# V turned on VectorE in a hybrid attention block on one core of a Trainium2

## The chip, the cores and the metric

The kernel runs on one core of one Trainium2 chip. The time is device microseconds of one execution, the median of several runs. A profile is one further execution, recorded by the hardware profiler. In its rows PE is TensorE, DVE VectorE, ACT ScalarE, POOL GpSimd and SP SyncE; L460 is line 460 of the kernel. All arithmetic is float32 or, for matrix operands, fp32r. Each product is made of three matmuls from a high and a low part of each operand (high × high, high × low, low × high).

## The reference, cut to what matters

One decoder layer with sequence 1024 and width 2048. A combined projection gives q, k, v and a gate for 8 stick-breaking heads (head dim 128) and 8 differential heads (two 64-wide q/k pairs, 128-wide v, rotary on a quarter of q and k). Each group's output is gated with SiLU, both are concatenated and projected, and a gated embedding and a final norm follow.

```python
hn = rmsnorm(h, norm_mix_g[i])
proj = hn @ w_in[i]                       # 1024x2048 @ 2048x8192
sb_q, sb_k, sb_v, sb_g, df_q, df_k, df_v, df_g = jnp.split(proj, split_at, axis=-1)
# stick-breaking: w = exp(log_sigmoid(z) + later), strictly causal; out = w @ v
# differential:   a = softmax1 - lam * softmax2, causal;             out = a @ v
df_out = rmsnorm(df_out, subln_g[i], 1e-5) * (1.0 - lambda_init)
mixed = jnp.concatenate([sb_out * silu(sb_g), df_out * silu(df_g)], axis=-1)
h = h + mixed @ w_out[i]
gate = sigmoid(rmsnorm(h, norm_ple_g[i]) @ w_ple_gate[i])
h = h + gate * (p[i] @ w_ple_proj[i])
return rmsnorm(h, norm_final_g)
```

The row norm is a factor per token, so v and the gate are projected from x times the gain alone and multiplied by the token's factor later.

## The kernel before

Activations lie feature by token: a tile holds 128 features in its partitions and 512 tokens (half a sequence, "half 1" and "half 0") along its free dimension. The kernel has four stages.

**Projection of v and gate (0 to about 650 us).** Class `Seven` computes it with seven instead of eight block products (a Strassen-like scheme). A unit u is one 128-column block, for v and gate and both halves. There are two phases over the inner dimension; phase 0 stores results into `vg_d` in DRAM and phase 1 adds to them there. In `prod` one product is 12 matmuls; `step` then makes a coming product's weight (`whigh` forms a difference on VectorE, L764, and casts it on ScalarE, L799; `wlow` makes the low part on VectorE, L811/L813) and runs what is due (`soon`, `xq`). Results leave PSUM in `evict` (L1017), in the loop over pairs (L1205 to L1217), in `second_result` (L1237), in `rest_of` (L1175) and after S3 (L1257); `vput` (L935) stores them through GpSimd's queue. Block 0 of `vg_d` is v, block 1 the gate; the half comes first. Tiles named `hc` share a ring of four buffers, "f".

**Heads (650 to about 1690 us).** For half 1 and then half 0, sixteen heads each: first the differential heads 8 to 15, then the stick-breaking heads 0 to 7. `unit` computes q and k of one head in four pieces with 96 matmuls and 32 ticks. `Side` holds the previous head's attention as functions with a due tick; `side.tick` runs them between matmuls. The tables at the top (`SC`, `TT`, `SVG`, `VGD`, `SBT`, `NORM_LAT` and others) are these due ticks, in steps of three matmuls. The orders of TensorE, VectorE and ScalarE follow the program text ("manual schedule"); those of GpSimd and of the DMA queues come from the scheduler. `load_vg` (L1505) fetches v and gate of a head; `normed` multiplies them by the tokens' factors `rstd`; `values` (L455) transposes v on TensorE in four 128x128 blocks into PSUM and splits it into high and low parts, token by feature. `turn` and `mix` transpose the attention weights and multiply them with v. For a differential head `norm` (L565) follows, with `roots` on ScalarE and `step` on VectorE. In half 0 the keys and values of half 1 come back as `k2` and `v2` (L1651 to L1664). `wprep` (L170) brings the weights: most heads' high and low parts lie ready in DRAM; those of the last two pieces of head 15 and of heads 0 to 7 in half 1 are made from a raw load (`high`, `low`, L188 to L195).

**Output projection (about 1690 to 2000 us).** `Seven` again, in two phases; in phase 1 the results are stored, summed (`sums`, L1782) and squared (`row_squares`, L1390, whose additions run on GpSimd, L1404).

**Gate, embedding and final norm (to the end).**

Of the kernel before, what the change touches and what calls it, by code (L numbers as in the profile page):

```python
# [20 lines left out]
P = 128  # L21
# [4 lines left out]
H = 8  # L26
# [8 lines left out]
SC = ((6.5, 7, 9.0, 11.5, 15.5, 17.5, 20.0, 21.5), (10.5, 10.5, 15.5, 22.5))  # L35
TT = ((19, 31, 17.5), (20.5, 36.5, 18))
# [3 lines left out]
LV = ((2.5, 2.5), (1, 2))  # L40
LT = ((1, 1), (1, 2.0))
LM = ((0.5, 2.0, 3, 5), (1.5, 2.5, 4.5, 6.5))
LN = ((1, 3.0), (1, 4.5))
PRIO = 300
NORM_LAT = ((11.0, 7.0), (13, 11))
XLAT = 5
SBB = ((20, 20, 15, 15.5, 16, 16.5, 16.5, 16.0), (20, 9, 5.5, 4, 4.5, 6.0, 5.5, 3.5))
SBS = ((-1, 3.5, 15.5, 23.5), (-2.5, 3, 7.0, 11.5))
# [5 lines left out]
ROPE = ((-1.4, 1.5, 3.0, 3.5, 2.7, 4.5, 6.0, 7.0), (-1.9, -1, 0, 1, 0.20000000000000018, 2, 3, 4))  # L54
ROPE_ = ((3.5, 4.0, 6.0, 10.0, 11.6, 12.5, 15.0), (6.5, 7, 9.5, 12.5, 12.6, 13.5, 14))
VGD = ((31, 37, 37.0, 39.0, 41.0), (22.5, 32.5, 35.5, 37.0, 45.0))
# [4 lines left out]
LAST = ((1.5, 4), (2, 4.0))  # L61
# [9 lines left out]
def _body(ctx, nc, tc, ap):  # L71
# [24 lines left out]
    lam = const.tile([P, 1], F32, name="lam", tag="lam")  # L96
    qzs = {}
# [72 lines left out]
    def wprep(wsrc, pc, half, hd):  # L170
# [22 lines left out]
        def low():  # L193
            V.tensor_tensor(lo, raw, hi.bitcast(F32), op=ALU.subtract)
            nc.sync.dma_start(wlo_d[hd, pc].bitcast(F32), lo.bitcast(F32))  # L195
# [111 lines left out]


    def attention(at, pz, half, hd, q, qz, K, KL, VV, sg, vg, state):
# [145 lines left out]
        def values():  # L455

            assert "v" in state
            vps = pp.tile([P, 4, P], F32, name="vps", tag="t")
            for j in range(4):
                T.transpose(vps[:, j, :], vg[0][:, j * P:(j + 1) * P], ident)  # L460
            v = at.tile([P, 2, 4, P], F32R, name="v", tag="v")
            side.later(1 if sb else LV[half][0], lambda: A.copy(v[:, 0], vps))

            def low():
                V.tensor_tensor(v[:, 1], vps, v[:, 0].bitcast(F32), op=ALU.subtract)
                VV.insert(0, v)
                if half == 1:
                    G.dma_start(v_d[hd], v.rearrange("p a b c -> p (a b c)"))

            side.later(2 if sb else LV[half][1], low)  # L470

# [93 lines left out]
        def norm(pr):  # L565
# [12 lines left out]
            def roots():  # L578
# [3 lines left out]
                A.activation(r, r, AF.Exp, scale=-0.5)  # L582

            def step():
                V.scalar_tensor_tensor(sg, sg, -0.5, r, op0=ALU.mult, op1=ALU.mult)
                A.activation(r, r, AF.Square)
# [36 lines left out]
    with tc.tile_pool(name="at", bufs=2) as at, ExitStack() as banks:  # L623
# [32 lines left out]
        class Seven:  # L656

            def __init__(self, w, n, flow):
# [7 lines left out]
                self.extra, self.ticks = (), False  # L666
# [166 lines left out]
            def step(self, taken=None):  # L833

                self.slot += 1
                self.whigh()
                if taken and not self.ticks:
                    taken()
# [95 lines left out]

        def vput(o, ph, hf, blk, u):  # L935
# [81 lines left out]
        def evict(n, u):  # L1017
            pool, tag, m = spots[u] if n == 3 else (ev, "f", 4)
            o = pool.tile([P, HALF], F32, name="s1", tag=tag, bufs=m)
            if u in (3, 5) and n == 3:  # L1020
# [154 lines left out]
        def rest_of(st_, first):  # L1175
# [6 lines left out]
            vput(o, ph, hf, blk, u)  # L1182
# [22 lines left out]
        for u in range(H, 2 * H, 2):  # L1205
            pair = []
            for nm in ("A11", "A12"):
                for j in range(2):
# [4 lines left out]
                    A.copy(o, pair[j])  # L1213
                    if nm == "A11":
                        G.dma_start(vgpart_d[u + j], o)
                    else:
                        vput(o, 0, 1, 0, u + j)  # L1217
        prev = None
        for ph in range(2):
            for u in range(2 * H):  # L1220
# [16 lines left out]
                def second_result():  # L1237
                    prod(u, ph, "A12", a, False)
                    o = ftile()
                    A.copy(o, a)  # L1240
# [56 lines left out]
        side.add([(4, norms)])  # L1297
        X0 = {}
# [79 lines left out]
        def gate_loads(nm, i0, n=4, eng=nc.sync):  # L1378
            e = [(op.slot + (3 if nm in ("A11", "A12") else 2), gate_operand(nm, i0 + j, eng)) for j in range(n)]
# [108 lines left out]
        for half in (1, 0):  # L1488
# [5 lines left out]
            for hd in (ORDER0, ORDER1)[half]:  # L1494
# [10 lines left out]
                def load_vg(vg=vg, hd=hd, half=half):  # L1505
                    for i in range(2):
                        vg.append(f32t(("vf", "gf")[i]) if hd < H else ev.tile([P, HALF], F32, name=("vf", "gf")[i], tag="xt", bufs=4))
                        with tc.issue_after(lastw[0].ins):
                            nc.sync.dma_start(vg[i], vg_d[half, i, hd])
# [47 lines left out]

                acc = two_accs()
                if sb:
# [18 lines left out]
                    def normed(i, vg=vg, rstd=rstd, state=state):  # L1578
                        V.tensor_tensor(vg[i], vg[i], rstd, op=ALU.mult)
# [8 lines left out]
                else:  # L1588
# [50 lines left out]
                    def normed(i, vg=vg, rstd=rstd, state=state):  # L1639
                        V.tensor_tensor(vg[i], vg[i], rstd, op=ALU.mult)  # L1640
# [781 lines left out]
```

## Time and profile before

| | us |
|---|---|
| median of 3 runs (lowest to highest) | 2362.04 (2360.44 to 2363.05) |
| profiled execution, its own time | 2361.19 |
| its span, first to last instruction | 2359.4 |
| TensorE busy | 2317.2 (98%) |
| VectorE busy | 1789.8 (76%) |
| ScalarE busy | 1189.0 (50%) |
| GpSimd busy | 327.3 (14%) |

The mean granted clock of TensorE was 0.997. In a group's row stand the line, engine, operation, the tile written and the tiles read, the shapes and the count; behind the first bar the busy time and the mean length of one in ns; behind the second how long the engine stood idle before such instructions, and what ended the idle time. A row of waits reads "who, on what: total us, times, longest us". Matmuls overlap one another, so a busy time is the union of their lengths.

### The profile page before, as it was taken

How to read it: one execution, taken by the hardware profiler on the slowest of the kernel's cores; microseconds unless marked ns; L12 is line 12 of the kernel's file. 1: busy time of each engine (PE TensorE's matmuls, PEld its weight loads, DVE VectorE, ACT ScalarE, POOL GpSimd, SP SyncE). 2: the span in 40 equal slices, each digit the busy share in tenths (PEclk: the TensorE clock that was granted, in tenths of full speed). 3: DMA queues.
4: the chain of work that ended last, by engine and by line, in shares of the span. 5: the costliest groups of instructions: out<-in, count | busy, mean ns of one | idle time of the engine just before them, and what ended most of it. 6: DMA issues, size and time to landing. Idle time of an engine off the chain costs nothing.

```text
span 2359.4 us, 32445 instructions
## 1 busy us (share of the span) xinstructions
PE 2317.2 (98%) x11096; PEld 1928.3 (82%) x11096; DVE 1789.8 (76%) x3123; ACT 1189.0 (50%) x2214; POOL 327.3 (14%) x480
## 2 busy tenths in 40 slices
PE   9999999999999999999999999999999999999997
PEld 7888888888888878887888888888878878788886
DVE  7489676666677787777888876767887877788778
ACT  6334243333367775445676764445633435533544
POOL 2211112332200000000001011011121232000000
PEclk9999999999999999999999999999999999999998
DMA  7699589999977788787656566677888778898666
GB/s 260 225 313 344 170 255 281 293 278 271 303 246 252 246 266 299 256 263 245 204 182 199 165 190 215 203 214 238 213 211 215 242 229 269 291 326 292 243 227 217
DMA packets 252725, 581.02 MB, mean 246 GB/s; under 512 B 28496, under 2 KB 41040, under 8 KB 252560
## 3 DMA queue, kind: packets, MB, share of 16 engines
q1 hardware_dynamic: 177952, 394.34, 49.7%
q0 software_dynamic: 55312, 149.71, 24.2%
q10 hardware_dynamic: 19296, 34.90, 4.3%
q8 instruction: 87, 1.43, 0.3%
q14 instruction: 78, 0.64, 0.1%
HBM read 373.32 MB, written 213.91 MB: 249 GB/s over the span
## 4 chain that ended last, share of the span: by engine, by line
PE 71%; DVE 12%; ACT 7%; DMA 6%; issue 3%; SPq 0%; ACTq 0%; DVEq 0%
PE acc L263 7%; PE acc L261 7%; PE acc L262 7%; PE pbc L708 6%; PE pbc L710 6%; PE pbc L709 6%; PE pa L708 2%; PE pa L710 2%; PE pa L709 2%; PE tp L480 2%; DMA wraw<-w_out 2%; PE pb L708 1%; PE pb L710 1%; PE pb L709 1%; PE pb L1941 1%
## 5 line engine op out<-in xcount | busy, mean ns | idle before, releaser
L799 ACT CAST wpr<-T 128x512 fp32r<-128x512 f32 x208 | 125.3, 621 | 440.3 <-DVE T L764 360.4
L261 PE MATMUL acc<-xh,whi 128*128 128x512 f32 x768 | 315.0, 410 | 0.0
L263 PE MATMUL acc<-xh,wlo 128*128 128x512 f32 x768 | 302.5, 394 | 1.5 <-DMA wlo<-wlo_d 1.4
L262 PE MATMUL acc<-xl,whi 128*128 128x512 f32 x768 | 301.0, 392 | 0.0
L263 PEld LDWEIGHTS acc<-xh,wlo 128*128 128x128 f32 x768 | 144.5, 188 | 36.2 <-DMA wlo<-wlo_d 3.6
L262 PEld LDWEIGHTS acc<-xl,whi 128*128 128x128 f32 x768 | 145.4, 189 | 24.0
L261 PEld LDWEIGHTS acc<-xh,whi 128*128 128x128 f32 x768 | 145.0, 189 | 23.4 <-DVE qk L1567 0.2
L799 ACT CAST wpr<-wraw 128x512 fp32r<-128x512 f32 x144 | 88.6, 618 | 146.9 <-DMA wraw<-w_vg 40.2
L813 DVE TENSOR_TENSOR wpr<-T,wpr 128x512 fp32r<-128x512 f32 x208 | 145.8, 701 | 9.2 <-ACT wpr L799 6.8
L936 POOL DMA_DIRECT2D vg_d<-hc x120 | 86.8, 724 | 328.4 <-DVE hc L1181 187.9
L503 DVE TENSOR_TENSOR awl<-tp,awh 128x256 fp32r<-128x256 f32 (+1 forms) x160 | 92.5, 578 | 42.8 <-ACT awh L498 42.2
L498 ACT CAST awh<-tp 128x256 fp32r<-128x256 f32 (+1 forms) x160 | 80.6, 504 | 82.6 <-PE tp L480 76.3
L813 DVE TENSOR_TENSOR wpr<-wraw,wpr 128x512 fp32r<-128x512 f32 x144 | 97.7, 686 | 23.5 <-ACT wpr L799 23.5
L321 DVE CUSTOM_DVE_ANT_0 z<-z,masks 128x512 f32<-128x512 f32 (+7 forms) x128 | 97.1, 769 | 23.0 <-PE z L341 14.0
L708 PE MATMUL pbc<-cS,wpr 128*128 128x512 f32 x288 | 112.0, 389 | 0.0
L709 PE MATMUL pbc<-cS,wpr 128*128 128x512 f32 x288 | 112.0, 389 | 0.0
L710 PE MATMUL pbc<-cS,wpr 128*128 128x512 f32 x288 | 112.0, 389 | 0.0
L373 DVE TENSOR_TENSOR_SCAN st<-pt 128x511 f32<-128x511 f32 (+3 forms) x64 | 86.7, 1354 | 27.2 <-ACT pt L366 26.8
L366 ACT ACTIVATE pt<-z 128x512 f32<-128x512 f32 (+3 forms) x64 | 41.8, 653 | 76.6 <-DVE z L349 74.6
L528 PE MATMUL av<-awl,v 128*128 128x256 f32 x256 | 73.4, 287 | 1.7 <-DVE awl L503 1.7
L526 PE MATMUL av<-awh,v 128*128 128x256 f32 x256 | 72.0, 281 | 0.7 <-ACT awh L498 0.7
L527 PE MATMUL av<-awh,v 128*128 128x256 f32 x256 | 72.2, 282 | 0.0
(589 smaller groups left out, 6816.5 us busy)
## 6 DMA issues: line engine op xcount, KB each, us to landing
wlo<-wlo_d SPq DMA_DIRECT2D x94, 512.0 KB, 5.2
whi<-whi_d SPq DMA_DIRECT2D x74, 512.0 KB, 4.1
wraw<-w_vg SPq DMA_DIRECT2D x129, 256.0 KB, 4.8
vg_d<-hc POOLq DMA_DIRECT2D x120, 256.0 KB, 5.7
wraw<-w_in SPq DMA_DIRECT2D x54, 512.0 KB, 5.3
wraw<-w_gate SPq DMA_DIRECT2D x92, 256.0 KB, 4.9
wraw<-w_out SPq DMA_DIRECT2D x72, 256.0 KB, 4.6
wlo_d<-wlo SPq DMA_DIRECT2D x34, 512.0 KB, 3.4
```

What stands on the lines that cost most here:

```text
L261: T.matmul(acc[c], hi[:, k2, kh, c, :], xh, start=first, stop=False)
L262: T.matmul(acc[c], hi[:, k2, kh, c, :], xl, start=False, stop=False)
L263: T.matmul(acc[c], lo[:, k2, kh, c, :], xh, start=False, stop=last)
L321: V.tensor_tensor_reduce(z, z, mwide[:, 0:n], -DF_SCALE, 3.0e38, ALU.add, ALU.min, mx)
L373: V.tensor_tensor_scan(st[:, off + 1:nkey], pt[:, off:nkey - 1], pt[:, off:nkey - 1], initial=1.0, op0=ALU.mult, op1=ALU.bypass)
L503: V.tensor_tensor(wl[:, o, :], tp[:, o, :], wh[:, o, :].bitcast(F32), op=ALU.subtract)
L708: T.matmul(o, wh[:, w], xh, start=start and k == 0, stop=False, skip_group_check=True)
L709: T.matmul(o, wh[:, w], xl, start=False, stop=False, skip_group_check=True)
L710: T.matmul(o, wl[:, w], xh, start=False, stop=k == 3, skip_group_check=True)
L799: A.copy(t[:, 0], src)
L813: V.tensor_tensor(t[:, 1], src, t[:, 0].bitcast(F32), op=ALU.subtract)
L936: G.dma_start(vg_d[hf, blk, u], o, **(dict(accum_op=ALU.add) if ph else {}))
```

## The change

**V is turned on VectorE.** Before it is stored, each tile of v (128 features by 512 tokens) goes through `vturn`: VectorE turns each 32x32 block and puts block (b, k) at place (k, b). Where ScalarE copied a result out of PSUM (`evict` for n > 3, the A12 results of the pairs, `second_result`), VectorE now turns it out of PSUM. In `rest_of` for the first result, the sum is written as before and turned into a second "f" tile two slots later, which is then stored. `load_vg` fetches v in four DMAs of 32 partitions each, in runs of 128 floats, so that it arrives token by feature. `values` no longer uses TensorE or PSUM; it casts and subtracts from the loaded tile. Since tokens are now in the partitions, v is multiplied by a column of factors, `rcol`, made once for each half by four transposes (`columns`, in the first unit). The gate is handled as before.

**Roots.** In `norm`, exponential and square both run in `roots` on ScalarE, into a separate tile; `step` on VectorE uses them.

**Six low parts.** `low` in `wprep` runs on GpSimd for heads 15 and 0 of half 1.

**Order.** Many due steps in the tables are moved. For the differential heads of half 0 from the third on, `k2` and `v2` are requested at steps 13 and 22 of their own unit instead of at its end. In phase 1 of the output projection the function handed to `prod` runs ahead of `whigh`, the last S1's sum is handed over that way, and the second half of `sums` comes one slot later. The first S2 loads of the gate stage are split one slot later.

```diff
-SC = ((6.5, 7, 9.0, 11.5, 15.5, 17.5, 20.0, 21.5), (10.5, 10.5, 15.5, 22.5))
-TT = ((19, 31, 17.5), (20.5, 36.5, 18))
+SC = ((6.5, 7, 9.0, 11.5, 15.5, 17.5, 20.0, 21.5), (10.5, 10.5, 15.5, 23.0))
+TT = ((19, 31, 16.0), (21.5, 36.5, 20))
...
-LN = ((1, 3.0), (1, 4.5))
+LN = ((1, 6.0), (1, 4.5))
...
-NORM_LAT = ((11.0, 7.0), (13, 11))
+NORM_LAT = ((8.0, 8.5), (13, 11))
...
-SBT = ((15, 31, 13), (16.0, 30.0, 11.5))
+SBT = ((15, 31, 13), (16.0, 30.0, 14.5))
...
-SVG = ((18, 37.5, 40, 40, 46), (34.5, 38.5, 41.0, 42.0, 49.5))
-CST = (19.5, 20)
+SVG = ((18, 37.5, 40, 40, 46), (30.5, 37.5, 41.0, 43.5, 49.5))
+CST = (16.5, 19.5)
...
-VGD = ((31, 37, 37.0, 39.0, 41.0), (22.5, 32.5, 35.5, 37.0, 45.0))
+VGD = ((19.5, 37, 37.0, 39.5, 44.0), (22.5, 32.5, 35.5, 37.0, 45.0))
...
+LOWG = ORDER1[H - 1:H + 1]
...
         def low():
-            V.tensor_tensor(lo, raw, hi.bitcast(F32), op=ALU.subtract)
+            (G if half and hd in LOWG else V).tensor_tensor(lo, raw, hi.bitcast(F32), op=ALU.subtract)
...
+    def blocks(t):
+        return t.rearrange("p (b k j) -> p b k j", b=4, k=4)
...
         def values():
-            vps = pp.tile([P, 4, P], F32, name="vps", tag="t")
-            for j in range(4):
-                T.transpose(vps[:, j, :], vg[0][:, j * P:(j + 1) * P], ident)
             v = at.tile([P, 2, 4, P], F32R, name="v", tag="v")
-            side.later(1 if sb else LV[half][0], lambda: A.copy(v[:, 0], vps))
+            hi, lo = [v[:, i].rearrange("p k (b j) -> p b k j", b=4) for i in range(2)]
+            raw = blocks(vg[0])
+            A.copy(hi, raw)
...
-                A.activation(r, r, AF.Exp, scale=-0.5)
+                sqs["root"] = ev.tile([P, HALF], F32, name="root", tag="ssq", bufs=1)
+                A.activation(sqs["root"], r, AF.Exp, scale=-0.5)
+                A.activation(r, sqs["root"], AF.Square)
...
-                A.activation(r, r, AF.Square)
...
+        def vturn(o, src):
+            V.transpose(blocks(o).rearrange("p b k j -> p k b j"), blocks(src))
...
+            if n > 3:
+                vturn(o, aa[u])
...
             V.tensor_tensor(o, o_, t, op=ALU.add)
-            vput(o, ph, hf, blk, u)
+            if not first:
+                return vput(o, ph, hf, blk, u)
+            def turned():
+                v = ftile()
+                vturn(v, o)
+                vput(v, ph, hf, blk, u)
+            if ph == 1 and u == 2 * H - 1:
+                turned()
+            else:
+                gv.soon.append((gv.slot + 2, turned))
...
+        def columns(hf):
+            ps = pp.tile([P, 4, P], F32, name="rps", tag="t")
+            for j in range(4):
+                T.transpose(ps[:, j, :], rstds[hf][:, j * P:(j + 1) * P], ident)
+            side.later(1, lambda: A.copy(rcol[:, hf, :], ps[:, :, 0]))
+        side.add([(20, partial(columns, 1)), (24, partial(columns, 0))])
...
-                            nc.sync.dma_start(vg[i], vg_d[half, i, hd])
+                            if i:
+                                nc.sync.dma_start(vg[i], vg_d[half, i, hd])
+                            for a in range(0 if i else 4):
+                                rows = slice(32 * a, 32 * a + 32)
+                                nc.sync.dma_start(vg[i][rows].rearrange("p (b e) -> p b e", b=4), vg_d[half, i, hd].rearrange("(b p) (a e) -> a p b e", b=4, a=4)[a])
...
+                            r = rcol[:, half, :].rearrange("p (b k j) -> p b k j", b=1, j=1)
+                            V.tensor_tensor(blocks(vg[i]), blocks(vg[i]), r.broadcast_to([P, 4, 4, 32]), op=ALU.mult)
...
-                    op.soon.extend((op.slot + lag + i, fn) for i, fn in enumerate(sums(...)))
+                    op.soon.extend((op.slot + lag + (1 + (lag == 1)) * i, fn) for i, fn in enumerate(sums(...)))
```

More of the change, by code (lines that the diff above doesn't have):

```diff
@@ L468, in low @@
                     G.dma_start(v_d[hd], v.rearrange("p a b c -> p (a b c)"))
-            side.later(2 if sb else LV[half][1], low)
+            side.later(1, low)
         def turn(pr, g):
@@ L1556, in gated, with load_second @@
                     V.tensor_tensor(sg, sg, vg[1], op=ALU.mult)
+                second = {}
+                if half == 0 and not sb and hd not in ORDER0[:2]:
+                    def load_second(nm, d, second=second, hd=hd):
+                        t = at.tile([P, 8 * P], F32R, name=nm, tag=nm)
+                        G.dma_start(t, d[hd])
+                        second[nm] = t
+                    side.add([(13, partial(load_second, "k2", k_d)), (22, partial(load_second, "v2", v_d))])
                 acc = two_accs()
```

75 lines of the change are left out of this document (46 added, 29 removed).

## The prediction

> **What bounds the kernel now.** I read the page's busy line and its chain of waits first.
>
> ```profile
> PE 2317.2 (98%) x11096; PEld 1928.3 (82%) x11096; DVE 1789.8 (76%) x3123; ACT 1189.0 (50%) x2214; POOL 327.3 (14%) x480
> ...
> PE 71%; DVE 12%; ACT 7%; DMA 6%; issue 3%; SPq 0%; ACTq 0%; DVEq 0%
> ```
>
> TensorE works through 98% of the span and carries most of the chain; its idle time is 2359.4 − 2317.2 = 42.2 us. A microsecond of matrix work removed is therefore worth nearly a microsecond, as long as no other engine falls behind. Busy time by stretches shows who could:
>
> ```profile
> 0.00:600.00 600.00, 595.69 (x2614) 491.10 (x2615) 426.90 (x646) 242.97 (x403) 137.52 (x223) 1.00 0.87 269
> ...
> 120.00:160.00 40.00, 40.00 (x178) 33.14 (x177) 34.04 (x56) 15.70 (x28) 6.51 (x12) 1.00 0.92 304
> 160.00:200.00 40.00, 40.00 (x178) 33.10 (x177) 36.80 (x59) 16.51 (x29) 9.23 (x17) 1.00 1.00 355
> 200.00:240.00 40.00, 40.00 (x178) 33.14 (x177) 35.33 (x58) 16.77 (x29) 4.88 (x9) 1.00 0.88 310
> ...
> 2330.00:2359.00 29.00, 14.35 (x100) 12.77 (x98) 20.95 (x46) 9.08 (x16) 0.00 (x0) 0.79 0.48 160
> ```
>
> The columns are TensorE, weight load, VectorE, ScalarE and GpSimd, then clock and DMA. VectorE (fourth number) is the next in line: 71% in the first 600 us, but 92% from 160 to 200. Of the 42.2 us, 14.7 lie in the last 29 us, which the change does not touch. TensorE's own waits, longest first:
>
> ```profile
> PE pbc L708 <- DVE u L1912: 3.5, 4, 1.5
> PE z L427 <- ACT et L439: 3.3, 4, 1.7
> PE acc L261 <- DVE qk L1567: 2.8, 1, 2.8
> ...
> PE acc L263 <- DVE wlo L194: 1.5, 1, 1.5
> ```
>
> The columns are the sum, how often and the longest. With 600 − 595.7 = 4.3 us in the first stretch, 42.2 − 14.7 − 4.3 = 23.2 us of waiting lie between 600 and 2330.
>
> **Step 1, transposes leave TensorE.** The change removes the four transposes of each of 32 calls of values(). Matmuls overlap, so I price a call by the starts around it, not by the length of one (columns: start, length, engine, line):
>
> ```profile
> 657.10 0.39 PE L263 MATMUL acc<-xh,wlo 128*128 128x512 f32 x1
> 657.33 0.60 PE L460 MATMUL vps<-ident,vf 128*128 128x128 f32 x4
> 657.69 0.48 PE L261 MATMUL acc<-xh,whi 128*128 128x512 f32 x1
> 658.00 0.40 PE L262 MATMUL acc<-xl,whi 128*128 128x512 f32 x1
> ```
>
> A 128x512 matmul starts 0.23 us after the last one. The L262 at 658.00 would put its predecessor's undisturbed start at 657.77, and the transposes began at 657.33: 0.44 us for four. 32 × 0.44 = **−14.1 us**. Added are two columns() calls, eight transposes, 8 × 0.11 = **+0.9**. They stand at steps 20 and 24 of the first unit, long after the norms they read (step 4).
>
> **Step 2, VectorE turns blocks.** 32 copies from PSUM by ScalarE (L1023, L1213, L1240) become VectorE turns, and 32 further turns follow the sums at L1181: 64 in the first 650 us. No block turn is in this trace. Bounds: a plain 128x512 VectorE copy from PSUM and the longest 512-column group. The nearest relative is the shuffle, which also reorders lanes inside groups of 32:
>
> ```profile
> 30.56 0.68 DVE L1021 COPY s<-paz 128x512 f32<-128x512 f32 x1
> ```
> ```profile
> L1606 DVE STREAM_SHUFFLE sw<-acc x32: 724/736/749, 640.3 to 1369.4; 128x512 f32<-128x512 f32 x32
> ```
> ```profile
> L373 DVE TENSOR_TENSOR_SCAN st<-pt 128x511 f32<-128x511 f32 (+3 forms) x64 | 86.7, 1354 | 27.2 <-ACT pt L366 26.8
> ```
>
> I take 0.74, between 0.68 and 1.35. The stage becomes 426.9 + 64 × 0.74 = 474 of 600 us. The tight place is 120 to 240: 178 matmuls in 40 us and 60 in a unit make 13.5 us a unit, so 8.9 turns fall in 120 us: 106.2 + 6.6 = 112.8, or 118.2 at the upper price. Both fit, so the sum gets 0. The cover is VectorE's slack; without it each turn costs its length. A turn out of PSUM waits for the last matmul of its product in VectorE's order, where ScalarE waited before; behind it stand the next low part (L813), for TensorE, and the next difference (L764), for ScalarE, both made one or two products (2.7 to 5.4 us) ahead. For the range I keep 0 to +3.
>
> **Step 3, V's loads, multiply and split.** Each V load becomes four, in 512-byte instead of 2-KB pieces. The multiply takes a per-row column (rcol), and the split reads SBUF instead of PSUM. I price both at their present length, on the grounds that they still pass 512 elements; a difference would lie in VectorE's slack here too. What can be late is the load:
>
> ```profile
> L1509 SPq DMA_DIRECT2D vf<-vg_d x32: 319/424/1072, 632.2 to 1628.3; - x32
> ...
> DMA to landing us min/median/max: 3.6/5.7/10.8
> ```
> ```profile
> q1 hardware_dynamic: 177952, 394.34, 49.7%
> ```
> ```profile
> 936.48 0.92 SPq L1509 DMA_DIRECT2D vf<-vg_d  x1
> ```
> ```profile
> 941.76 0.67 DVE L1579 TENSOR_TENSOR vf<-vf,ssa 128x512 f32<-128x512 f32 x1
> ```
>
> Three more issues are 3 × 0.42 = 1.3 us of the SP queue, in front of the G load and the next weights. Queue 1 spends 0.497 × 16 × 2359.4 / 177952 = 0.105 us on a packet, so 384 more packets over 16 engines cost between nothing and 2.5 us: landing after 5.7 to 9.5 us. In the stick-breaking heads of half 1 the margin is 5.3 us; the change issues four steps earlier and multiplies one step earlier, three steps or 2.1 us at 3 × 0.23 a step. So it lands between in time and 2.1 us late, in eight heads. I take 0, since most of the added packets share the engines with nothing ahead of them, and keep +17 (8 × 2.1) as the far end. The page "DMA: Bandwidth & Descriptors" of the Trainium skill (Why small descriptors are slow) gives about three bus cycles of overhead a packet; at 32 bytes a cycle that makes 19 against 16.75 cycles per 512 bytes, an estimate of 13% more, and the load would stay in time. No run here shows it.
>
> **Step 4, six low parts on GpSimd.** Heads 15 and 0 of half 1 leave VectorE's L194.
>
> ```profile
> L194 DVE TENSOR_TENSOR wlo<-wraw,whi x34: 1200/1224/1227, 826.2 to 1063.7; 128x1024 fp32r<-128x1024 f32 x34
> ```
> ```profile
> L1404 POOL TENSOR_TENSOR total<-total,masks 128x512 f32<-128x512 f32 x15 | 19.8, 1322 | 39.6 <-ACT masks L1403 32.9 <-DMA hr<-h_d 4.3 <-DMA b<-w_out 2.4
> ```
> ```profile
> 859.12 1.23 DVE L194 TENSOR_TENSOR wlo<-wraw,whi 128x1024 fp32r<-128x1024 f32 x1 [0.35 <-ACT whi L189]
> 860.26 0.69 DVE L321 CUSTOM_DVE_ANT_0 z<-z,masks 128x512 f32<-128x512 f32 x1
> ```
> ```profile
> 903.93 0.69 DVE L587 SCALAR_TENSOR_TENSOR msqs<-msqs,rsub 128x512 f32<-128x512 f32 x1 [0.76 <-ACT rsub L586]
> ...
> 905.27 1.22 DVE L194 TENSOR_TENSOR wlo<-wraw,whi 128x1024 fp32r<-128x1024 f32 x1
> 906.40 0.68 DVE L1567 TENSOR_TENSOR qk<-acc,ssa 128x512 f32<-128x512 f32 x1
> ```
>
> VectorE sheds six times 1.22; GpSimd needs 2 × 1.32 = 2.64 each. Twice (826 and 859) an L194 stands right before the masking whose exponentials (L439) hold TensorE, 3.3 us in four waits, and once before the L1567 that holds it for 2.8: 1.1 each, 3.4 together. There L587 also waits 0.76 for the square (L586) that the change puts straight behind the exponential. The 1.5 us wait on L194 itself I leave as it is: an earlier start, a longer run. That makes 3.4 + 0.8 = −4.2. Against it stands contention:
>
> ```profile
> L1792 DVE SCALAR_TENSOR_TENSOR hq<-hc,gvec,hq 128x512 f32<-128x512 f32 x6 | 7.7, 1276 | 19.2 <-ACT hq L1791 19.2
> ```
> ```profile
> L1088 DVE SCALAR_TENSOR_TENSOR xv<-xv,gvec 128x512 f32<-128x512 f32 x4 | 3.0, 751 | 0.2
> ```
>
> The same kind of instruction takes 1276 ns beside L1404 and 751 ns where GpSimd does no arithmetic: 0.53 given back per part, 6 × 0.53 = 3.2 on VectorE, of which I let 1.2 reach TensorE. Net **−3.0**, bounds −8 (every wait around the seam gone) to +11 (rival 2). "GPSIMD Engine Reference" of the Trainium skill (Key points) warns of just this contention for VectorE instructions with two SBUF inputs; by it the move of low parts should be left alone, and the term would be 0 or a loss. The trace agrees on the contention.
>
> **Step 5, roots and output projection.** The square moves on ScalarE only. VectorE no longer waits for it in the middle of its step:
>
> ```profile
>   ACT rsub L586: 13.2, 16
> ```
>
> That is 0.8 us a head on an engine with slack, 0 beyond the 0.76 already counted. In the second phase of the output projection the second half of sums() goes one slot later:
>
> ```profile
> 1918.15 0.74 DVE L1798 SCALAR_TENSOR_TENSOR hq<-hq,gneg 128x512 f32<-128x512 f32 x1
> 1918.93 0.75 DVE L1800 SCALAR_TENSOR_TENSOR hc<-hc,gneg,hq 128x512 f32<-128x512 f32 x1
> 1919.60 0.69 DVE L1912 TENSOR_TENSOR u<-pbc,s 128x512 f32<-128x512 f32 x1
> ```
>
> These two, 1.45 us, stand ahead of L1912, whose four waits sum to 3.5 and are 1.5 at most: **−3.0** (0 to −3.5). What comes later are the two stores behind them, which nothing reads for many slots.
>
> **Step 6, the moved steps and earlier k2/v2 loads.** Those loads are not among TensorE's waits, so 0; GpSimd's queue only meets them earlier, when their buffers are free. For the retimed steps I take **+1**: no row prices an order not yet run. Bounds are −11, which is 23.2 − 3.5 − 8 of waits that are left, and as much the other way, +11.
>
> **Sum**: −14.1 + 0.9 − 3.0 − 3.0 + 1.0 = −18.2. The profiled execution took 2361.19 us (span 2359.4), 0.85 below the median shown: 2361.2 − 18.2 + 0.85 = **2343.8**.
>
> **Rivals.**
> 1. Freed time comes back as waiting. TensorE waits in many units already; where it waits later in the same unit, a call's 0.44 is lost. If 20 of 32 are, 8.8 return: 2352.6. For it: one call's transposes stand directly before the 2.8 us wait on L1567, which ends no sooner without them.
>
> ```profile
> 903.83 0.60 PE L460 MATMUL vps<-ident,vf 128*128 128x128 f32 x4
> 907.23 0.47 PE L261 MATMUL acc<-cA11h,whi 128*128 128x512 f32 x1 [2.80 <-DVE qk L1567]
> ```
>
> Against: 23.2 us of waiting are too few for 20 of 32 calls to have a long one behind them. In the extreme, where no wait at all shrinks and all calls are followed by one, the removal would do nothing.
> 2. GpSimd's parts cost more than they free: if its 2.64 us shut VectorE out, VectorE loses 6 × (2.64 − 0.75) = 11.3, and step 4 is +11 instead of −3: 2343.8 + 14 = 2357.8, no change that can be measured. For it: GpSimd's order is not written by hand, and a part behind a store of v waits with it.
>
> ```profile
> POOL v_d L468 <- DVE v L465: 155.7, 14, 17.1
> ```
> ```profile
> L813 DVE TENSOR_TENSOR wpr<-T,wpr x24: 684/690/1376, 1860.3 to 1968.7; 128x512 fp32r<-128x512 f32 x24
> ```
>
> Against: beside L1404, a 128x512 instruction of VectorE took at most 1.38 us, and the median stayed at 0.69.
> 3. Slower: V lands late at L1579 in the eight stick-breaking heads of half 1, VectorE stops in order, and the low parts and q/k behind it stop TensorE. It turns the sign when each head loses over (18.2 + 4.7) / 8 = 2.9 us, that is when landing passes 5.3 + 2.1 + 2.9 = 10.3 us. The old maximum was 10.8; with 3.8 on top, 14.6, each loses 7.2: 2343.8 + 58 = 2401. Against: the median is 5.7.
> 4. The retiming also clears most remaining waits: −11 instead of +1, 2332.
>
> **Chances.** Forecast 0.55 (own range 2337 to 2351), rival 1 0.12, rival 2 0.12, rival 3 0.09, rival 4 0.12. A measurement of this kernel tells 0.2%, 4.7 us, from no change. The forecast and rivals 1 and 4 are faster: 0.79; rival 2 same: 0.12; rival 3 slower: 0.09. The range 2333 to 2360 leaves out rival 3 and half of rival 4.
>
> **What would show it.** Step 1: no vps group, eight rps transposes, TensorE's busy time near 2304. Step 2: 64 turns at 0.74 and no new wait in 60 to 650. Step 3: no VectorE wait on vf beyond 1 us. Step 4: GpSimd low parts near 2.6 us, the waits on L439 and L1567 smaller. Step 5: no wait on L1912. Wrong: a total of TensorE waits above 26 us, or turns above 1.4 us.

## The result, and the profile after

The changed kernel takes 2346.62 us (median of 6 runs, 2343.15 to 2348.8), against 2362.35 us for the kernel before (6 runs, 2360.44 to 2363.78). The ratio is 0.9936, with a 95% interval of 0.9926 to 0.9945: 15.7 us less. The forecast was 2343.8. The profiled execution took 2344.73 us, its span is 2342.9.

The busy line and the chain of waits of the changed kernel, from its page:

```profile
PE 2300.4 (98%) x10976; PEld 1916.2 (82%) x10976; DVE 1828.0 (78%) x3181; ACT 1170.5 (50%) x2184; POOL 345.4 (15%) x486
...
PE 76%; DMA 10%; DVE 8%; ACT 4%; issue 1%; SPq 0%; ACTq 0%; DVEq 0%
```

TensorE's busy time fell by 16.8 us (2317.2 to 2300.4); its idle time is 42.5 us, as the 42.2 before. So the whole gain stands in the busy column. That does not mean that the waits did not matter: what they were is not what they are now. TensorE's longest waits after (sum, times, longest):

```profile
PE pbc L713 <- DVE u L1968: 5.2, 5, 1.9
PE acc L265 <- DMA wlo<-wlo_d: 4.7, 8, 1.1
PE z L341 <- ACT k L1619: 2.2, 1, 2.2
PE acc L263 <- DVE qk L1611: 1.6, 1, 1.6
...
PE z L432 <- ACT et L444: 1.3, 1, 1.3
```

The waits on the exponential (et, 3.3 before) and on qk (2.8 before) shrank, the one on u grew (3.5 before), and one on the low parts of weights that come by DMA (wlo<-wlo_d, 1.4 before) is new in size.

To see in which stage the time was saved, take the first matmul of the heads' projections (the second row's first start) and the last round of them (the first row's last start). Line 261 of the kernel before is line 263 of the changed one. The kernel before:

```profile
L261 PE MATMUL acc<-xh,whi x768: 387/395/628, 631.4 to 1644.5; 128*128 128x512 f32 x192
L261 PE MATMUL acc<-cA11h,whi x128: 387/389/798, 618.8 to 1051.8; 128*128 128x512 f32 x128
```

The changed kernel:

```profile
L263 PE MATMUL acc<-xh,whi x768: 387/393/628, 632.2 to 1626.0; 128*128 128x512 f32 x192
L263 PE MATMUL acc<-cA11h,whi x128: 387/389/799, 619.5 to 1041.3; 128*128 128x512 f32 x128
```

The heads take 1644.5 − 618.8 = 1025.7 us before and 1626.0 − 619.5 = 1006.5 after. That is 19.2 us less, more than the whole gain (the two spans differ by 16.5); the stages before them are the same within 0.7 us, and those behind them are longer (before 2359.4 − 1644.5 = 714.9, after 2342.9 − 1626.0 = 716.9). This length of the heads is used below for every kernel.

### The profile page after: what moved, and what is told of

Its sections match the earlier page's. It is cut to its first block, busy times and chain, and to the rows that moved or that the text cites. A ratio compares the mean times of both kernels' runs of the same rounds, so it can differ in the third digit from the quotient of the medians.

```text
span 2342.9 us, 32443 instructions
## 1 busy us (share of the span) xinstructions
PE 2300.4 (98%) x10976; PEld 1916.2 (82%) x10976; DVE 1828.0 (78%) x3181; ACT 1170.5 (50%) x2184; POOL 345.4 (15%) x486
## 4 chain that ended last, share of the span: by engine, by line
PE 76%; DMA 10%; DVE 8%; ACT 4%; issue 1%; SPq 0%; ACTq 0%; DVEq 0%
PE acc L265 8%; PE acc L263 8%; PE acc L264 8%; PE pbc L713 6%; PE pbc L715 6%; PE pbc L714 6%; DMA wlo<-wlo_d 3%; PE pa L714 2%; PE pa L713 2%; PE pa L715 2%; PE tp L484 2%; DMA wraw<-w_gate 2%; DMA wraw<-w_out 2%; PE pb L715 1%; PE pb L713 1%
## 5 line engine op out<-in xcount | busy, mean ns | idle before, releaser
L378 DVE TENSOR_TENSOR_SCAN st<-pt 128x511 f32<-128x511 f32 (+3 forms) x64 | 86.7, 1354 | 23.5 <-ACT pt L371 22.5
```

What stands on the lines that cost most here:

```text
L378: V.tensor_tensor_scan(st[:, off + 1:nkey], pt[:, off:nkey - 1], pt[:, off:nkey - 1], initial=1.0, op0=ALU.mult, op1=ALU.bypass)
```

## The experiments

Each ratio is to the kernel before, measured beside it on the same chip (medians there 2360.7 to 2361.45); differences in us are between those medians. Lengths of the heads, busy times and waits are those of the one profiled execution. It can lie some us from the median of its kernel, most with the square on VectorE (9.2 above), the low parts on VectorE (8.8 above) and V with the new steps (4.5 above), so that small differences between such figures say little.

**The transposes taken out of the kernel before.** V is split as it lies, so that this kernel computes something else.

```diff
-            vps = pp.tile([P, 4, P], F32, name="vps", tag="t")
-            for j in range(4):
-                T.transpose(vps[:, j, :], vg[0][:, j * P:(j + 1) * P], ident)
+            vps = vg[0].rearrange("p (b c) -> p b c", b=4)
```

> The kernel before with nothing changed but that values() leaves out the 128 transposes of v on TensorE and splits v as it lies (feature by token), so the attention multiplies with another arrangement of v. It prices step 1 alone. Theory (a matmul-bound kernel gives the time back): 14.1 us less, ratio 0.9940, TensorE busy near 2303, waits of TensorE about as before (42 us idle). Rival 1 (freed time comes back as waiting): 5 us less, ratio 0.998, TensorE busy 2303 but its idle time up to about 51 us. Without the removal mattering at all: ratio 1.000.

Measured: 2351.8 us, ratio 0.9959 (0.9942 to 0.9975), 8.9 us less, between the two expectations. TensorE's busy time fell by 13.1 us, to 2304.1, and its idle time rose by 4.1, to 46.3. The heads take 1020.0 us, 5.7 less. Nearly as long as the added idle time is one wait that the kernel before had once, for 0.2 us (waits of TensorE in this kernel):

```profile
PE z L340 <- ACT et L397: 4.2, 8, 0.8
```

**V turned on VectorE, and nothing else.** The turns, the load in four pieces, rcol and columns() as in the change; times, roots, low parts, sums and the loads of k2 and v2 as before.

> V turned on VectorE and loaded in four pieces, rcol and its eight transposes, but everything else as before: the old due steps, low parts on VectorE, roots and sums as before, k2 and v2 loads at the old place. Theory: 13.2 us less (ratio 0.9944), 64 turns of 0.71 us, TensorE's wait on wlo from DRAM stays near 1.4 us and its wait on u (output projection) near 3.5 us. Rival (the new waits of the changed kernel on wlo, 4.7 us, belong to V's four-piece load): 10 us less, with that wait at 4 to 5 us. Rival (old steps do not suit the new loads): V late at its multiply in the stick-breaking heads of half 1, over 1 us a head, 0 to 5 us less.

Measured: 2360.92 us, ratio 0.9998 (0.9988 to 1.0007). The heads take 1025.7 us, to the tenth what they took before, with 128 transposes fewer. In a span of 2359.4 us, as before, TensorE's busy time is 11.0 us less (2306.2) and its idle time 11.0 us more (53.2). TensorE's waits between 1100 and 1400, where the differential heads of half 0 run, in the kernel before:

```profile
PE acc L263 <- DMA wlo<-wlo_d: 1.4, 2, 0.9
...
PE z L340 <- ACT et L397: 0.2, 1, 0.2
```

and with V turned alone:

```profile
PE acc L265 <- DMA wlo<-wlo_d: 4.9, 4, 1.4
PE z L345 <- ACT et L402: 4.0, 8, 0.7
```

Eight differential units, eight waits of half a microsecond on the exponential: the 0.44 us that a call of values() gave up there come back as a wait later in the same unit. These are 3.8 of the 11.0 us; the wait on wlo grew by 4.3 in the whole kernel (1.4 to 5.7), and the rest is spread over others. The outcome is that of rival 1, in full. But the wait on the exponential alone does not explain it: where the transposes were only left out it is as long, and 8.9 us were gained. V was not late either: VectorE waited for it twice, 1.6 us in all. So the change's gain needs something beside V.

**The second half of the sums back where it was.**

```diff
-                    op.soon.extend((op.slot + lag + (1 + (lag == 1)) * i, fn) for i, fn in ...
+                    op.soon.extend((op.slot + lag + i, fn) for i, fn in ...
```

> The changed kernel with the second half of sums() in its old slot (one earlier). Theory, after the trace: the move of sums made things worse, because its stores now stand in SP's queue ahead of weight loads; undone, TensorE's waits on u fall from 5.2 to 3.5 us or below, SP's waits on L1854 fall from 16 to about 9 us, and the time is 2 to 4 us lower (ratio to before near 0.992). As predicted before the result: undone, L1854 and L1856 stand ahead of u again and 3 us are lost (ratio 0.995). If the function ahead of whigh is to blame, nothing changes.

Measured: 2347.28 us, ratio 0.9938 (0.9923 to 0.9954), the changed kernel's own. The waits on u in the output projection are 4.0 us instead of 5.2, but the move of the sums does nothing to the time that can be measured.

**All low parts on VectorE.**

```diff
-            (G if half and hd in LOWG else V).tensor_tensor(lo, raw, hi.bitcast(F32), op=ALU.subtract)
+            V.tensor_tensor(lo, raw, hi.bitcast(F32), op=ALU.subtract)
```

> The changed kernel with all low parts on VectorE again. Prediction: the six GpSimd parts give 3 us (ratio 0.995 instead of 0.9936); TensorE's waits between 820 and 910 us grow from 4.5 to about 8 us. Rival 2 (GpSimd's parts cost what they free): no change within 1 us. If they cost more: faster by up to 3 us.

Measured: 2345.94 us, ratio 0.9929 (0.9913 to 0.9946). GpSimd's six parts do nothing that can be measured either. TensorE's waits between 820 and 910 are 5.8 us here, against 4.6 in the changed kernel and 8 expected.

**V turned and the new steps, without the low parts and the new roots.** The changed kernel with the edit above and, in norm():

```diff
-                sqs["root"] = ev.tile([P, HALF], F32, name="root", tag="ssq", bufs=1)
-                A.activation(sqs["root"], r, AF.Exp, scale=-0.5)
-                A.activation(r, sqs["root"], AF.Square)
+                A.activation(r, r, AF.Exp, scale=-0.5)
...
-                V.scalar_tensor_tensor(sg, sg, -0.5, sqs["root"], op0=ALU.mult, op1=ALU.mult)
+                V.scalar_tensor_tensor(sg, sg, -0.5, r, op0=ALU.mult, op1=ALU.mult)
+                A.activation(r, r, AF.Square)
```

> The changed kernel with the six low parts back on VectorE and the roots and the step after them as before: V turned and the new order are left. If these two edits do nothing singly or together: 2346.6 within 2. If the low parts and the roots cover for one another (each alone may be absorbed): 2349 to 2352, with waits of a microsecond and more on ScalarE's exponential or on VectorE's weights at the seam near 820 to 910.

Measured: 2360.86 us, ratio 1.0 (0.999 to 1.0009). Both expectations were far off: the whole gain is gone. Since the low parts alone cost nothing, it is the roots: 2345.94 with the new ones, 2360.86 with the old. The heads take 1643.8 − 619.9 = 1023.9 us. Where a part of the 15 us arises is seen in one differential unit of half 0. ScalarE with the old roots (start, length, engine, line; in brackets the idle time before it):

```profile
1197.28 0.72 ACT L585 ACTIVATE rsub<-msqs,eps 128x512 f32<-128x512 f32 x1
1198.03 0.63 ACT L586 ACTIVATE rsub<-rsub 128x512 f32<-128x512 f32 x1
1199.43 0.63 ACT L590 ACTIVATE rsub<-rsub 128x512 f32<-128x512 f32 x1 [0.76 <-DVE sg L589]
1199.96 0.88 ACT L402 ACTIVATE et<-z,mx 128x768 f32<-128x768 f32 x1
```

and TensorE in the same stretch:

```profile
1200.99 0.39 PE L345 MATMUL z<-k,q 128*128 128x256 f32 x1 [0.48 <-ACT et L402]
```

The square (L590) cannot start before VectorE has read the root that it overwrites (L589). ScalarE stands 0.76 us, and behind the square in its order is the exponential L402, which reads z; TensorE may write z again only after it, and waits 0.48 us. With the new roots the same unit reads:

```profile
1188.88 0.71 ACT L585 ACTIVATE rsub<-msqs,eps 128x512 f32<-128x512 f32 x1
1189.63 0.63 ACT L587 ACTIVATE root<-rsub 128x512 f32<-128x512 f32 x1
1190.29 0.63 ACT L588 ACTIVATE rsub<-root 128x512 f32<-128x512 f32 x1
1190.83 0.89 ACT L402 ACTIVATE et<-z,mx 128x768 f32<-128x768 f32 x1
```

From the start of L585 to that of the exponential it is 1190.83 − 1188.88 = 1.95 us, against 1199.96 − 1197.28 = 2.68 with the old roots: 0.73 us earlier, and TensorE's L345 does not wait for it. Over the heads, the waits with the old roots were:

```profile
PE acc L265 <- DMA wlo<-wlo_d: 7.5, 7, 2.0
PE z L432 <- ACT et L444: 6.7, 6, 2.4
PE z L345 <- ACT et L402: 3.2, 7, 0.5
```

against 4.7, 1.3 and none in the changed kernel: 11.4 us, of 1023.9 − 1006.5 = 17.4. TensorE's busy time is longer too, 2306.4 against 2300.4 us for as many matmuls. How the old roots come to lengthen the wait on wlo is not shown.

**The new steps and roots with V on TensorE.** The changed kernel with values(), the load, the copies and the multiply of V as before.

> The changed kernel with V transposed on TensorE, copied by ScalarE and loaded as one piece, as before; its other steps, times, low parts and roots stay as changed. V turned alone gave nothing (2360.9 against 2360.7 of the kernel before) and all of it together gave -15.7. Theory A, the order alone clears waits: the heads stage shortens as it did with the change, and the time is about 2346 with TensorE busy some 14 us longer and waiting some 14 us less. Theory B, both are needed, because the new order only keeps TensorE from giving the freed 0.44 us per transpose group back as waits: about 2360, TensorE busy near 2318 and waiting near 42 as before. Between 2350 and 2356 each has a share of its own.

Measured: 2358.34 us, ratio 0.9987 (0.9975 to 0.9999), 2.8 us less; heads 1024.7. Theory B: TensorE is busy for 2314.4 us, 14.0 more than in the changed kernel, and idle for 44.7, against 42.5. V's transposes have waits of their own in the new order:

```profile
PE msq L574 <- DVE v L470: 4.1, 2, 2.1
```

Both lie before 1100. msq and the transposed V share the PSUM buffers of one tag ("t"), and the norm's matmul waits there until VectorE has read V out.

**Half 0's, then half 1's times as before.** In each table of times the one half's tuple is put back, as in

```diff
-NORM_LAT = ((8.0, 8.5), (13, 11))
+NORM_LAT = ((11.0, 7.0), (13, 11))
```

> The changed kernel with the times of half 0's heads as before (V loaded at step 31 rather than 19.5 there, the normalisation's and the rotation's steps as before); half 1's times stay as changed. With V turned and all times as before, the differential units of half 0 took 37.9 to 40.1 us, in the changed kernel 36.9 to 37.5: eight units. If half 0's times carry the gain: about 2355, with the waits on the exponential and on the weights' low parts back behind 1100. If they are worth nothing: 2346.6 within 2.

> The changed kernel with the times of half 1's heads as before; half 0's stay as changed. With V turned and all times as before, half 1's differential units took 28.67 us against 28.25 in the changed kernel, seven units: 3 us, and the two units at the seam 63.7 against 60.2. If half 1's times carry that: 2350 to 2353, with L527 again waiting on its lead in each differential unit. If the gain is half 0's alone: 2346.6 within 2.

Measured: half 0 put back 2355.84 us, ratio 0.9981 (0.9972 to 0.9991), heads 1017.0; half 1 put back 2353.78 us, ratio 0.997 (0.9959 to 0.9981), heads 1013.4. Both halves' times count: half 0's for 9.2 us, as expected, half 1's for 7.2 (each against 2346.62), just outside the range that was expected. With half 0 put back, the waits between 1100 and 1400 are 6.7 us on wlo (4.2 in the changed kernel) and 1.1 on the exponential (none there). With half 1 put back, the wait of the line L527 on its lead, which was to come back in each unit, is 0.4 us in all; a part of the loss lies at the seam between the two kinds of heads, where between 820 and 910 the waits were

```profile
PE acc L263 <- DVE qk L1611: 3.9, 2, 3.1
PE acc L263 <- DVE sw L1654: 2.4, 1, 2.4
```

against 1.6 on qk and none on sw in the changed kernel, and 2.8 and 0.6 in the kernel before.

**The new roots alone, and V with the new roots.** The kernel before, and the kernel with V turned alone, each with the three lines of norm() as changed.

> The kernel before with the new roots alone (exponential and square one after the other on ScalarE, into two tiles): V on TensorE and all steps as before. It takes away VectorE's 13.2 us of waiting on the square and ScalarE's 7.3 us of waiting on VectorE, in 16 heads. Theory A, the hand-over back and forth holds up what stands behind it on both engines wherever it is: 2350 to 2354. Theory B, while TensorE still turns V it is the bound there and the stall is covered: 2359 to 2362.

> V turned on VectorE and the new roots; all steps, times, low parts and loads of k2 and v2 as before. V alone gave nothing; V with the new steps but the old roots gave nothing either (2360.9). Theory A, the roots are what holds V's gain back, and the new steps matter little: 2346 to 2350. Theory B, all three are needed together: 2356 to 2360. The half-and-half runs (half 0's old times 2355.8, half 1's old times 2353.8, each with the new roots) speak for something near 2357 if their losses of 9.2 and 7.2 were to add.

Measured: roots alone 2356.28 us, ratio 0.9976 (0.9966 to 0.9986), 5.2 us less, heads 1023.5; this lies between the two theories. V and roots 2355.45 us, ratio 0.9974 (0.9964 to 0.9983), 6.0 us less, heads 1016.4, just beside theory B. The eight waits on the exponential that V alone had left are down to a quarter (waits between 1100 and 1400 with V and roots):

```profile
PE acc L265 <- DMA wlo<-wlo_d: 4.3, 5, 1.1
...
PE z L345 <- ACT et L402: 0.9, 5, 0.2
```

The waits on the weights' low parts stay.

**The new steps alone.** V on TensorE, old roots, low parts on VectorE.

> The new steps alone: V on TensorE and loaded as before, roots as before, low parts on VectorE; the times, the moved loads of k2 and v2 and the later second half of the sums as changed. With the new roots and the low parts on GpSimd the same order gave 2358.3. If the order is worth nothing without the other two: 2358 to 2363. If it costs where roots are old, since the step after the roots now comes half a unit earlier on VectorE and waits longer there: above 2363.

Measured: 2370.79 us, ratio 1.0041 (1.0026 to 1.0055), 9.3 us more; heads 1029.4. The order of the change is a loss without the two edits that it was set for. Its waits on the exponential of half 1's heads are those of the order with the old roots above, 6.7 us, in six waits, twice the 3.3 of the kernel before. The same order with the new roots has 1.3 there with V turned, and 1.2 with V on TensorE.

**The square on VectorE.** The changed kernel; ScalarE neither squares nor waits, VectorE does one operation more in each head.

```diff
-                A.activation(r, sqs["root"], AF.Square)
...
+                V.tensor_tensor(r, sqs["root"], sqs["root"], op=ALU.mult)
                 V.scalar_tensor_tensor(sg, sg, -0.5, sqs["root"], op0=ALU.mult, op1=ALU.mult)
```

> The changed kernel with the square taken by VectorE instead of ScalarE, as the first operation of the step (16 more VectorE operations of about 0.69 us; no hand-over back to VectorE). With the roots as before the same kernel was 15 us slower, and there VectorE stood 0.7 us and ScalarE 0.6 to 0.8 us in each head. If VectorE's lost time is the price: about 2357 to 2361, since 0.69 us of work stands where 0.71 us of waiting stood. If ScalarE's standing behind VectorE is the price: 2344 to 2348, since ScalarE here neither waits nor squares.

Measured: 2355.41 us, ratio 0.9979 (0.9967 to 0.999), 6.0 us less than before, between the two expectations. Of the 14.5 us that the old roots cost (14.8 − 0.3), 16 operations of VectorE bring back 9.7 (15.7 − 6.0) with no hand-over at all. So the larger part of the price seems to be VectorE's lost time, and something like 5 us ScalarE's standing. This is no clean split: ScalarE also has 16 squares less to do, and the runs of this kernel spread over 13 us (2351.13 to 2364.57), and the profiled execution was the longest of them.

The runs on V, roots and steps form a table. Times are differences from the kernel before; the heads' length is that of the profiled execution. New steps are everything that the change lists under order: the tables of times, the earlier loads of k2 and v2, and the moves in the output projection. The last two rows also carry GpSimd's low parts, which the run on these found to be worth nothing.

| V turned | new roots | new steps | time, us | heads, us |
|---|---|---|---|---|
| no | no | no | 0 | 1025.7 |
| yes | no | no | +0.2 | 1025.7 |
| no | yes | no | −5.2 | 1023.5 |
| no | no | yes | +9.3 | 1029.4 |
| yes | yes | no | −6.0 | 1016.4 |
| yes | no | yes | −0.3 | 1023.9 |
| no | yes | yes | −2.8 | 1024.7 |
| yes | yes | yes | −15.7 | 1006.5 |

One by one the three edits sum to +4.3; together they give −15.7. Taken out of the changed kernel, each costs most of the gain: V 12.9, the roots 14.5 and the steps 8.8 (these two against the run with the low parts on VectorE, −14.8, where they have theirs too).

## Why the prediction was right, and where it was not

The time was right: 2346.6 in a range of 2333 to 2360, 2.8 above the forecast. The reasons were right in part only: the low parts, the sums, the roots and the steps were each priced wrongly, and that errors of both signs cancelled in the sum is luck.

**Step 1, the transposes** (−14.1 + 0.9). The size holds under a condition that the prediction did not name. The transposes are gone (nothing writes vps any more) and the eight of columns() are there:

```profile
L1326 PE MATMUL rps<-ident,ssa x8: 270/272/275, 635.6 to 639.1; 128*128 128x128 f32 x8
```

TensorE's busy time was to be near 2304 and is 2300.4. All waits of TensorE between 600 and 2314 come to 42.5 − 4.4 (first 600 us) − 14.6 (last 29 us, rows under step 2) = 23.5 us, as before and under the 26 that would have spoken against the forecast. In the changed kernel V is worth 12.9 us, close to the term. In the order of before the transposes left out are worth 8.9 us and V turned on VectorE nothing. The prediction put rival 1 (freed time comes back as waiting) at 0.12, with the ground that 23.2 us of waiting are too few; but the waits that took V's gain were short before (0.2 us on the exponential, 1.4 on wlo). A list of the waits of before cannot show them. What might have shown the first is the order on ScalarE: how long before TensorE needs z its exponential ends.

**Step 2, the turns** (0). Right. They were priced at 0.74 us and take 0.71:

```profile
L943 DVE STREAM_TRANSPOSE hc<-hc 128x512 f32<-128x512 f32 x32 | 22.6, 705 | 1.5 <-DMA vg_d<-hc 1.5
L943 DVE STREAM_TRANSPOSE hc<-pa 128x512 f32<-128x512 f32 x24 | 17.1, 712 | 11.8 <-PE pa L715 11.7
```

VectorE's first 600 us and its tightest 40 (fourth number; the last row is the end of the kernel):

```profile
0.00:600.00 600.00, 595.59 (x2610) 490.40 (x2611) 460.90 (x706) 226.83 (x372) 137.81 (x223) 1.00 0.86 268
...
160.00:200.00 40.00, 40.00 (x178) 33.15 (x177) 38.51 (x63) 16.30 (x29) 8.68 (x16) 1.00 1.00 359
...
2314.00:2343.00 29.00, 14.38 (x100) 12.75 (x98) 20.94 (x46) 9.20 (x16) 0.00 (x0) 0.77 0.46 161
```

460.9 us against 474 expected, and TensorE is busy all of the 40 us in which VectorE has 38.5. Between 60 and 650 both kernels have a single wait of TensorE, 0.9 us on u: no new wait.

**Step 3, V's loads** (0, to +17). Right, and rival 3 (V lands late) did not come. The pieces land after:

```profile
L1545 SPq DMA_DIRECT2D vf<-vg_d x128: 302/430/1508, 633.0 to 1612.1; - x128
...
DMA to landing us min/median/max: 1.9/4.5/7.8
```

This is each quarter from its own issue. A whole load, from its first issue to the last of its four landings, takes 5.7 us in the median and 9.1 at most in the same trace, against 5.7 and 10.8 before; 5.7 to 9.5 was predicted. VectorE waited for vf once, 0.8 us. But the change also moves the issue steps. With V turned alone, where these are the old ones, a whole load takes 6.5 us in the median and 11.6 at most. By the Trainium skill's page "DMA: Bandwidth & Descriptors" (Why small descriptors are slow) the smaller pieces were to take longer, by an estimated 13%; 6.5 against 5.7 is 14%, though the three further issues are in it too. The load was not put back by itself, so that its share in TensorE's waits on wlo is open.

**Step 4, GpSimd's low parts** (−3.0). The trace has what was predicted, and the time does not. They take 2.40 us each (2.64 predicted):

```profile
L196 POOL TENSOR_TENSOR wlo<-wraw,whi x6: 2361/2398/2802, 823.0 to 861.9; 128x1024 fp32r<-128x1024 f32 x6
```

TensorE's waits between 820 and 910 after the change:

```profile
PE acc L263 <- DVE qk L1611: 1.6, 1, 1.6
PE z L432 <- ACT et L444: 1.3, 1, 1.3
PE z L432 <- ACT k L1681: 1.1, 1, 1.1
PE acc L265 <- POOL wlo L196: 0.6, 1, 0.6
```

That is 4.6 us, and in the kernel before:

```profile
PE z L427 <- ACT et L439: 3.0, 2, 1.7
PE acc L261 <- DVE qk L1567: 2.8, 1, 2.8
PE acc L263 <- DVE wlo L194: 1.5, 1, 1.5
PE acc L261 <- DVE sw L1606: 0.6, 1, 0.6
```

7.9 us: 3.3 less, where 3.0 were forecast. But with all low parts on VectorE these waits are 5.8 us, so that 2.1 of the 3.3 come from other edits, and the time was 2345.94 us against 2346.62: the 1.2 that are left do not show in it. Most of the credit was given to the wrong edit. The Trainium skill ("GPSIMD Engine Reference", Key points) warns of contention with VectorE instructions that read two SBUF inputs, and by it this step would be 0 or a loss: 0 is what was measured, as rival 2 also had it for this step, though not with the loss that it priced.

**Step 5, the roots** ("0.8 us a head on an engine with slack, 0"). This is the term that was mis-sized: it measures −5.2 by itself and about −14.5 in its place. The prediction quoted the row that showed it, 13.2 us of VectorE waiting for the square in 16 heads, and set it aside because VectorE has slack over the whole. An engine that works in a fixed order has slack only until the next thing that TensorE needs from it. Two such things can stand behind the step: on ScalarE, which waited 7.3 us for VectorE in the same exchange, the exponential, as the unit above shows; and on VectorE the low parts and masks, for which only the run with the square on VectorE speaks. ScalarE's half of the exchange was not looked at. The rows, before:

```profile
DVE msqs L587 <- ACT rsub L586: 13.2, 16, 1.5
...
ACT rsub L586 <- DVE sg L585: 7.3, 9, 0.9
```

After, neither is left; VectorE waits for the root itself, as it did before (8.8 us then):

```profile
DVE sg L591 <- ACT root L587: 9.5, 11, 5.4
```

**Step 5, the sums** (−3.0 on L1912). Wrong. The waits on u are 5.2 us, not 0, against 3.5 before, and putting the sums back leaves the time as it is. The second half did move out of the way of u, but into another's. The changed kernel, then the kernel before:

```profile
L1856 DVE SCALAR_TENSOR_TENSOR hc<-hc,gneg,hq x8: 751/1656/1669, 1842.1 to 1995.6; 128x512 f32<-128x512 f32 x8
```
```profile
L1800 DVE SCALAR_TENSOR_TENSOR hc<-hc,gneg,hq x8: 752/752/753, 1859.0 to 2012.5; 128x512 f32<-128x512 f32 x8
```

One slot later five of the eight run beside GpSimd's L1436 and take 1.65 to 1.67 us instead of 0.75. With the sums put back all eight take 0.75 again, and the waits on u are still 4.0 us. So the larger part of these waits has another cause. In the kernels with the old order of the output projection they are 2.1 to 3.5 us, in those with the new one 4.0 to 6.0. The function that now runs ahead of whigh is one candidate; it was not tried by itself.

**Step 6, the moved steps** (+1, between −11 and +11). Mis-sized, and both bounds were needed: −8.8 with V and the new roots there, +9.3 without them. "No row prices an order not yet run" was right; to add it as a term of its own was the error, since an order has a worth only beside the durations that it is made for. The earlier loads of k2 and v2 were not tried apart from the tables.

**What stays open.** TensorE's waits on the low parts that come by DMA (wlo<-wlo_d) are 4.7 to 8.8 us in every kernel with V turned (4.7 in the changed kernel, 5.7 with V alone, 6.5 with V and the roots, 7.5 with V and the steps), and 0.8 to 4.6 in those without it (1.4 before, 1.9 with the transposes left out, 0.8 with the steps alone, 4.6 with the roots alone). So they go with V's new path more than with a faster TensorE, and the load in four pieces, which is part of that path, is a candidate that was not tried. Nor is it settled why V turned alone gave 9.1 us less than the transposes simply left out (2360.92 against 2351.8). Of the waits, that on wlo is the one that grew most between the two, from 1.9 to 5.7; the two kernels differ also in the turns, in how v is multiplied and in when it is copied.

## What to carry to other kernels

Before removing work from the bounding engine, look in the order of each engine that feeds it for what would be late next, and by how much; a wait that the trace shows as 0.2 us can grow to 4 and take a good part of the gain. An exchange back and forth between two engines (one waits for the other to have read before it overwrites) holds up everything behind it on both, and a second tile takes it away: here it was worth as much in its place as V's turn off TensorE (14.5 and 12.9 us), and that turn was worth something only with it and the new steps together. Test edits that were made together by taking each out as well as by putting each in: the single effects here sum to +4.3 us, the joint one is −15.7.

## What the runs showed of the hardware

After some waits TensorE is slower for a while. In the changed kernel, between 1060 and 1070 TensorE was busy 7.53 of 10 us (it waited 2.2 us on k), and in the next 10 us the granted clock was 0.83; the next again had 1.00 (the columns are as in the prediction, the clock last but two):

```profile
1060.00:1070.00 10.00, 7.53 (x38) 5.94 (x36) 4.97 (x9) 4.10 (x9) 0.02 (x1) 1.00 1.06 364
1070.00:1080.00 10.00, 10.00 (x41) 8.22 (x41) 9.71 (x18) 5.37 (x11) 0.51 (x1) 0.83 0.91 309
1080.00:1090.00 10.00, 10.00 (x51) 8.35 (x50) 7.21 (x16) 3.92 (x10) 2.39 (x3) 1.00 0.60 153
```

In stretches of 2 us the clock is 0.56 and 0.59 between 1070 and 1074 and 1.00 after. Eight 128x512 matmuls in a row start 0.43 us apart there, instead of 0.23, so that this wait of 2.2 us costs nearer to 4, and the second part of it stands in the busy column. The same followed a wait of 1.9 us on u at 1903 and, in the kernel before, one of 1.5 us at 1078. It is no rule of the length: the longest wait of the kernel before, 2.8 us on qk before 907, was followed by matmuls 0.23 us apart at a clock of 1.00, and at a clock of 1.00 it went on after the other waits of 1 to 2 us between 600 and 2310 too, six in the changed kernel and seven in the kernel before. What decides is not shown here. Where it happens, a removed wait shows as less busy time as well.

Arithmetic of GpSimd can more than double a VectorE instruction with two inputs in SBUF that runs beside it (L1856 above: 1.65 to 1.67 us in the five that ran beside L1436, 0.75 in the three that did not). A turn of 128x512 fp32 in blocks takes VectorE 0.71 us, whether it reads PSUM or SBUF, no longer than the shuffle of the kernel before (0.74).
